# New state of the chunked RWKV scan: the old state's unit-matrix product on TensorE against a scaled copy on ScalarE and one fused VectorE instruction

## The chip, the cores and the metric

The kernel runs on one core of one Trainium2 chip. Its engines are TensorE (PE, matrix products; the loading of its stationary operand is listed apart as PEld), VectorE (DVE), ScalarE (ACT), GpSimd (POOL) and SyncE (SP, which here issues most DMAs). Each engine works through its own list of instructions in order, and engines wait for each other by semaphores. The metric is the device time of one execution in microseconds (us). The profile comes from one further execution, taken by the hardware profiler.

## What is computed

The program is a two-layer encoder over 1280 tokens (a prompt of 256 and a sample of 1024), 1024 channels, float32. Layer 0 mixes tokens by a bidirectional RWKV-7 recurrence, layer 1 by neighbourhood attention; each is followed by a squared-ReLU MLP. Only the recurrence matters here. For each head (64 channels) and each direction it is

```
def step(S, inp):
    r_t, w_t, k_t, v_t, a_t, b_t = inp
    sa = jnp.einsum('bhvk,bhk->bhv', S, a_t)
    S = S * w_t[:, :, None, :] + sa[..., None] * b_t[:, :, None, :] + v_t[..., None] * k_t[:, :, None, :]
    return S, jnp.einsum('bhvk,bhk->bhv', S, r_t)
```

The kernel does not go token by token. It takes chunks of 64 tokens: within a chunk, products of 64 x 64 matrices give the outputs and the new state S from the old one. If the inputs of a chunk are scaled by the running decay, the new state is D * (S + K'v + B'u), where D is the decay of the whole chunk (one number per key channel, thus one per partition), v are the values, u is the solution of a triangular system of the chunk, and K' and B' are the chunk's scaled keys.

## The kernel before

**Stages.** Layer 0's projections come first, then the preparation of scaled operands for the scan (written to DRAM as `ar_d` and `bk_d`), then the scan, then the MLP of layer 0, the attention and the MLP of layer 1. The scan's recurrence runs from about 738 us to 1378 us of the span.

**Jobs and units.** The scan has ten jobs (`jobs`). Jobs 0 and 1 hold the prompt (four head pairs of 4 chunks each), jobs 2 to 9 hold one head pair of the sample each (16 chunks). A head pair fills the 128 partitions: a helper `pair` (its matmul is line 976) issues each product twice, for partitions 0 to 63 and 64 to 127, on two quarters of the array. A float32 product stands as two records per half in the trace, so one `pair` is four MATMUL records.

**The planner's clock.** All work of the scan is entered by `at(t, f)` with a due time t in units; job j starts at 16 j, and a unit holds one chunk forward (d = 0) and one chunk backward (d = 1, 0.481 later). `scan_until` sorts all entries by due time and emits them under a manual schedule, so each of PE, DVE, ACT and POOL executes its instructions exactly in that order. The due time sets the order only; the clock on the chip is whatever the engines make of it.

**A step of the recurrence** is `scan_step`, in four parts at t - 0.68, t, t + 0.33 and t + 0.66. They work in a PSUM tile `wu` per direction with three regions `w`, `us`, `sn`:

- `s0`: `w` = zk v.
- `s1`: `w` += ar S (the old state); ACT copies `w` to `up` (line 997); `yo` += zk v.
- `s2`: `yo` += ar S; `sn` = lt v (line 1006); `sn` += I S, the unit matrix `ident` times the old state (lines 1007 and 1008, in the trace `wu<-S,cst`); `us` = Q up; ACT copies `us` to `u` (line 1011).
- `s3`: `sn` += lt u; ACT writes the new state S = D * `sn` (line 1019, `dall` holds D); `yo` += zb u. Every fourth chunk of d = 1, DVE takes the output `yo` out (lines 1026 and 1028).

The next chunk's `s1`, 0.34 units after `s3`, is the first reader of the new state.

**What else runs in these units.** DVE masks the products of the coming chunks (`zk` line 928 and, after an ACT copy of the same PSUM tile at line 814, `zb` line 815) and normalises outputs (`scan_post`: sums, an inverse square root with two ACT steps at lines 1121 and 1122, lines 1053 to 1073 and 1109 to 1125), with three large tensor operations of it on POOL. Above all it inverts the triangular systems of the next job by 31 rank-one updates (`rank1`, lines 853 and 855: tmp = column * row, q += tmp). They are due from -16.24 of their own job, that is from -0.24 of the job that is scanned at the time, in batches every half unit, over about ten units. After them ACT transposes q (`qst`, line 868), SP stores it, loads it back in another layout (`qld`, lines 886 and 891) and goes on with the loads of `ar` (line 801) that stand behind in its queue.

Of the kernel before, what the change touches and what calls it, by code (L numbers as in the profile page):

```python
# [5 lines left out]
F32 = mybir.dt.float32  # L6
F32R = mybir.dt.float32r
AF = mybir.ActivationFunctionType
ALU = mybir.AluOpType
# [4 lines left out]
P = 128  # L14
# [4 lines left out]
L = 64  # L19
# [29 lines left out]
class Trunk:  # L49
# [722 lines left out]
    def at(self, t, f, level=3):  # L772
        self.todo.append((t, len(self.todo), f, level))
# [196 lines left out]
    def half(self, e):  # L970
        return slice(64 * e, 64 * e + 64)
# [6 lines left out]
    def scan_step(self, at, t, J, st, d, cc, m, ch, new, end, i, last):  # L978
        nc = self.nc
        g, c = cc // 4, cc % 4  # L980
        R = {}
        w, us, sn = (lambda s=s: self.pbank[d][:, s] for s in (slice(0, L), slice(L, 2 * L), slice(2 * L, 3 * L)))
        yb = lambda: self.ybank[i // 4 % 2]
        yo = lambda: yb()[:, int(g > 1), c, :]
        half = self.half

        def s0():
            zk, vt = J["zk"][d, g], J["vt"]
            self.pair(lambda e, z: (w()[z], zk[z, c, 0:64], vt[z, 0, cc, :]))

        def s1():
            ar, zk, vt = J["ar"][d, g], J["zk"][d, g], J["vt"]
            S = R["S"] = None if new else st["S"]
            if S is not None:
                self.pair(lambda e, z: (w()[z], ar[z, c, 0:64], S[z]), start=False, free=True)
            up = R["up"] = self.sp.tile([P, L], F32, name="up", tag="up", bufs=4)
            nc.scalar.copy(up, w())
            self.pair(lambda e, z: (yo()[half(1 - e)], zk[z, c, 64:128], vt[z, 0, cc, :]), start=d == 0 and i % 4 == 0, free=True)

        def s2():  # L1000
            Q, up, S, ar, vt = J["Q"], R["up"], R["S"], J["ar"][d, g], J["vt"]
            if S is not None:
                self.pair(lambda e, z: (yo()[half(1 - e)], ar[z, c, 64:128], S[z]), start=False, free=True)
            if not end:
                lt = J["lt"][d, g]
                self.pair(lambda e, z: (sn()[z], lt[z, c, 1, :], vt[z, 0, cc, :]), start=False, free=True)
                if S is not None:
                    self.pair(lambda e, z: (sn()[z], self.ident[z, z], S[z]), start=False, free=True)
            self.pair(lambda e, z: (us()[z], Q[z, cc, d, :], up[z]), start=last, free=True)
            u = R["u"] = self.sp.tile([P, L], F32, name="u", tag="u", bufs=4)  # L1010
            nc.scalar.copy(u, us())

        def s3():
            u, zb, y = R["u"], J["zb"][d, g], J["y"]
            if not end:
                lt = J["lt"][d, g]
                self.pair(lambda e, z: (sn()[z], lt[z, c, 0, :], u[z]), start=False, free=True)
                S2 = self.sp.tile([P, L], F32, name="S", tag="S", bufs=5)
                nc.scalar.activation(S2, sn(), AF.Copy, scale=self.dall[:, m, d, ch:ch + 1])
                st["S"] = S2  # L1020
            self.pair(lambda e, z: (yo()[half(1 - e)], zb[z, c, 64:128], u[z]), start=False, free=True)
            if d == 1 and i % 4 == 3:
                lo = min(g, 3 - g)
                y = y.rearrange("p (x c) v -> p x c v", c=4)[:, lo:4 - lo:3 - 2 * lo]
                if i < 8:
                    nc.vector.tensor_copy(y, yb())
                else:
                    nc.vector.tensor_tensor(out=y, in0=yb(), in1=y, op=ALU.add)
        at(t - 0.68, s0)
        at(t, s1)  # L1030
        at(t + 0.33, s2)
        at(t + 0.66, s3)

    def scan_post(self, at, J, grp, last):
# [865 lines left out]
```

## Time and profile before

| | |
|---|---|
| median of 3 runs | 4070.0 us (4069.32 to 4076.52) |
| the profiled execution | 4072.58 us, its span 4070.8 us |
| mean granted TensorE clock over the span | 0.965 |
| the scan's recurrence, 738 to 1378 us | 640 us |

The profile lists busy time by engine, groups of equal instructions by line with their mean duration, what each engine waited for, and single instructions in order of time. "Busy" of PE is the union of modelled spans that overlap, so the distance from one matmul's start to the next says more about its price than its duration. All products of `pair` share line 976; they are told apart by their tiles (`wu<-S,cst` is out `wu`, moving operand S, stationary operand from the constants).

### The profile page before, as it was taken

The page shows a single profiled execution, that of the slowest core. Times are in us where ns is not written, and L with a number is a line of the kernel's source. Part 1 is how long each engine was busy: PE and PEld are TensorE (multiplying, and loading weights), DVE is VectorE, ACT ScalarE, POOL GpSimd, SP SyncE. Part 2 cuts the span into 40 slices and gives each one's busy share as a digit, 9 for nine tenths or more (in the row PEclk, how much of TensorE's full clock was granted, in tenths as well). Part 3 has the DMA queues.
Part 4 walks back from the last instruction along what each step waited for, and adds up shares of the span by engine and source line. Part 5 has one row for each costly group of instructions (what it writes and reads, how often), then busy time and mean ns, then how long its engine had stood idle before and what let it go on. Part 6 is the DMA issues. An engine that isn't in the chain of part 4 may idle for free.

```text
span 4070.8 us, 91014 instructions
## 1 busy us (share of the span) xinstructions
PE 3830.8 (94%) x36820; PEld 3236.5 (80%) x36820; DVE 2236.7 (55%) x4581; ACT 1582.2 (39%) x3868; POOL 1337.9 (33%) x1252
## 2 busy tenths in 40 slices
PE   8988988788888899999999999999989999999999
PEld 5765578688888788888888879887778888888888
DVE  5777742465665447555555562355554755555555
ACT  6776642455555531111111133456663211111111
POOL 4445542022221434222222241344442422222222
PEclk9987889899999999999999999999999999999999
DMA  4226564666664431111111115345464111111101
GB/s 142 71 101 213 195 213 128 161 160 161 154 166 117 138 109 37 42 37 37 42 37 37 42 51 165 115 106 113 94 171 157 42 37 37 42 37 37 42 32 63
DMA packets 450885, 394.89 MB, mean 97 GB/s; under 512 B 267456, under 2 KB 352832, under 8 KB 450464
## 3 DMA queue, kind: packets, MB, share of 16 engines
q1 hardware_dynamic: 416048, 327.72, 28.5%
q10 hardware_dynamic: 34416, 61.35, 4.2%
q8 instruction: 289, 4.73, 0.5%
q14 instruction: 132, 1.08, 0.1%
HBM read 270.50 MB, written 124.44 MB: 97 GB/s over the span
## 4 chain that ended last, share of the span: by engine, by line
PE 79%; DVE 6%; ACT 5%; DMA 4%; issue 3%; POOL 2%; SPq 1%; ACTq 0%; DVEq 0%; POOLq 0%
PE ps L95 19%; PE ps L96 19%; PE ps L97 18%; PE wu L976 4%; PE vps L510 2%; PE vps L512 1%; PE vps L511 1%; PE op L1815 1%; PE aps L976 1%; PE kps L976 1%; PE pt L1758 1%; PE lps L976 1%; DVE q L855 1%; PE yo L976 1%; PE yps L976 1%
## 5 line engine op out<-in xcount | busy, mean ns | idle before, releaser
L1361 DVE TENSOR_TENSOR x<-ps,x 128x256 f32<-128x256 f32 x1488 | 814.4, 594 | 645.3 <-PE ps L97 645.0
L95 PE MATMUL ps<-ah,whi 128*128 128x512 f32 (+1 forms) x2304 | 842.6, 366 | 0.0
L96 PE MATMUL ps<-al,whi 128*128 128x512 f32 (+1 forms) x2304 | 825.9, 358 | 0.0
L97 PE MATMUL ps<-ah,wlo 128*128 128x512 f32 (+1 forms) x2304 | 823.2, 357 | 1.7 <-DVE wlo L90 1.4
L90 POOL TENSOR_TENSOR wlo<-raw,whi 128x1024 fp32r<-128x1024 f32 (+1 forms) x178 | 390.6, 2195 | 855.5 <-ACT whi L89 831.1
L95 PE MATMUL ps<-hh,whi 128*128 128x512 f32 (+1 forms) x1536 | 547.8, 357 | 9.4 <-DVE x L1361 9.4
L96 PE MATMUL ps<-hl,whi 128*128 128x512 f32 (+1 forms) x1536 | 546.7, 356 | 0.0
L97 PE MATMUL ps<-hh,wlo 128*128 128x512 f32 (+1 forms) x1536 | 545.9, 355 | 0.0
L95 PEld LDWEIGHTS ps<-ah,whi 128*128 128x128 f32 x2304 | 434.3, 189 | 72.6 <-issue 8.0
L97 PEld LDWEIGHTS ps<-ah,wlo 128*128 128x128 f32 x2304 | 433.4, 188 | 72.2 <-DVE wlo L90 1.9
L96 PEld LDWEIGHTS ps<-al,whi 128*128 128x128 f32 x2304 | 434.5, 189 | 62.9 <-issue 1.0
L89 ACT CAST whi<-raw 128x1024 fp32r<-128x1024 f32 (+1 forms) x206 | 200.5, 973 | 713.7 <-PE ps L96 630.1
L1340 POOL TENSOR_TENSOR rl<-rl 128x512 f32<-128x512 f32 (+1 forms) x192 | 174.2, 907 | 505.7 <-PE ps L97 462.3
L95 PEld LDWEIGHTS ps<-hh,whi 128*128 128x128 f32 x1536 | 291.5, 190 | 54.0 <-DVE x L1361 11.4
L97 PEld LDWEIGHTS ps<-hh,wlo 128*128 128x128 f32 x1536 | 291.7, 190 | 41.8
L96 PEld LDWEIGHTS ps<-hl,whi 128*128 128x128 f32 x1536 | 291.4, 190 | 40.6
L1339 ACT ACTIVATE rl<-ps 128x512 f32<-128x512 f32 (+1 forms) x192 | 100.8, 525 | 555.6 <-PE ps L97 555.6
L1342 ACT CAST hh<-rl 128x512 fp32r<-128x512 f32 (+1 forms) x192 | 105.6, 550 | 324.1 <-POOL rl L1340 324.1
L1343 DVE TENSOR_TENSOR hl<-rl,hh 128x512 fp32r<-128x512 f32 (+1 forms) x192 | 119.8, 624 | 143.6 <-ACT hh L1342 143.2
L1752 POOL TENSOR_TENSOR s<-s,mx 128x384 f32<-128x384 f32 (+1 forms) x150 | 109.9, 746 | 162.9 <-DVE mx L1751 114.7
L976 PE MATMUL aps<-ar,bb 64*64 64x128 f32 x1280 | 117.9, 290 | 24.2 <-DMA ar<-ar_d 17.6
L1057 POOL TENSOR_TENSOR y<-y,mu 128x512 f32<-128x512 f32 x18 | 19.3, 1075 | 368.1 <-DVE mu L1054 341.5
(302 smaller groups left out, 8288.5 us busy)
## 6 DMA issues: line engine op xcount, KB each, us to landing
raw<-in_w_down_dram SPq DMA_DIRECT2D x64, 512.0 KB
raw<-in_w_up_dram SPq DMA_DIRECT2D x64, 512.0 KB
ar<-ar_d SPq DMA_DIRECT2D x80, 256.0 KB
bk<-bk_d SPq DMA_DIRECT2D x80, 256.0 KB
ar_d<-ar ACTq DMA_DIRECT2D x32, 512.0 KB
bk_d<-bk ACTq DMA_DIRECT2D x32, 512.0 KB
bs<-tab SPq DMA_DIRECT2D x128, 96.0 KB
v_d<-vt ACTq DMA_DIRECT2D x80, 128.0 KB
```

The costliest lines, as they stand in the source:

```text
L89: nc.scalar.copy(hi[:, cs], raw)
L90: lo_eng.tensor_tensor(out=lo[:, cs], in0=raw, in1=hi[:, cs].bitcast(F32), op=ALU.subtract)
L95: mm(ps, sh, mh, start=first, stop=False)
L96: mm(ps, sh, ml, start=False, stop=False)
L97: mm(ps, sl, mh, start=False, stop=last)
L976: self.nc.tensor.matmul(out, w, x, start=start, stop=stop, skip_group_check=free)
L1339: nc.scalar.activation(r[:, :n], ps[:, :n], AF.Relu)
L1340: nc.gpsimd.tensor_tensor(out=r[:, :n], in0=r[:, :n], in1=r[:, :n], op=ALU.mult)
L1342: nc.scalar.copy(hh[:, :n], r[:, :n])
L1343: nc.vector.tensor_tensor(out=hl[:, :n], in0=r[:, :n], in1=hh[:, :n].bitcast(F32), op=ALU.subtract)
L1361: nc.vector.tensor_tensor(out=xv, in0=ps[:, :n], in1=xv, op=ALU.add)
L1752: nc.gpsimd.tensor_tensor(out=s[:, :nk], in0=s[:, :nk], in1=mx[:, 2:3].to_broadcast([P, nk]), op=ALU.mult)
```

## The change

The unit-matrix product leaves TensorE. In `s2` ScalarE multiplies the old state in SBUF by D into a new tile `sd` (three buffers, 128 x 64). In `s3` VectorE makes the new state: D times `sn`, plus `sd`, in one scalar_tensor_tensor instruction; where there is no old state (a first chunk), it is D times `sn` alone. ScalarE's instruction of line 1019 goes.

```
             if not end:
                 lt = J["lt"][d, g]
                 self.pair(lambda e, z: (sn()[z], lt[z, c, 1, :], vt[z, 0, cc, :]), start=False, free=True)
-                if S is not None:
-                    self.pair(lambda e, z: (sn()[z], self.ident[z, z], S[z]), start=False, free=True)
+            if S is not None and not end:
+                sd = R["sd"] = self.sp.tile([P, L], F32, name="sd", tag="sd", bufs=3)
+                nc.scalar.activation(sd, S, AF.Copy, scale=self.dall[:, m, d, ch:ch + 1])
             self.pair(lambda e, z: (us()[z], Q[z, cc, d, :], up[z]), start=last, free=True)
...
                 S2 = self.sp.tile([P, L], F32, name="S", tag="S", bufs=5)
-                nc.scalar.activation(S2, sn(), AF.Copy, scale=self.dall[:, m, d, ch:ch + 1])
+                if R["S"] is None:
+                    nc.vector.tensor_scalar(out=S2, in0=sn(), scalar1=self.dall[:, m, d, ch:ch + 1], scalar2=None, op0=ALU.mult)
+                else:
+                    nc.vector.scalar_tensor_tensor(out=S2, in0=sn(), scalar=self.dall[:, m, d, ch:ch + 1], in1=R["sd"], op0=ALU.mult, op1=ALU.add)
                 st["S"] = S2
```

Over the ten jobs this is 256 unit-matrix products (chunks with an old state and a successor), 256 new ScalarE instructions, and 288 new states that pass from ScalarE to VectorE (32 of them without an old state).

## Prediction

> **What bounds the kernel now.** I read the page's busy times first, then busy time by stretch for the scan, because only the scan is touched. Columns of the second fence: stretch, length, then busy time (and instructions) of PE, PEld, DVE, ACT, POOL, granted clock, DMA share, GB/s.
>
> ```profile
> span 4070.8 us, 91014 instructions
> ...
> PE 3830.8 (94%) x36820; PEld 3236.5 (80%) x36820; DVE 2236.7 (55%) x4581; ACT 1582.2 (39%) x3868; POOL 1337.9 (33%) x1252
> ```
>
> ```profile
> 738.00:1378.00 640.00, 561.27 (x18613) 521.99 (x18609) 365.37 (x914) 371.84 (x1387) 154.06 (x174) 0.97 0.60 148
> ```
>
> Over the scan PE seems to be the bound: 561 of 640 us, DVE only 365. But the rank-one updates fill ten of a job's sixteen units, so I cut the scan at their first and last instruction: nine stretches with them (742 to 776, 805 to 840 and so on to 1265 to 1301), eight without them between these, and the end. The two sum rows are of the nine and of the eight.
>
> ```profile
> 742.00:776.00 34.00, 31.17 (x1012) 29.54 (x1012) 25.66 (x71) 18.12 (x71) 0.00 (x0) 0.95 0.61 154
> ...
> 999.00:1038.00 39.00, 35.86 (x1176) 34.06 (x1178) 32.02 (x82) 20.65 (x80) 7.93 (x9) 0.94 0.58 143
> 1067.00:1104.00 37.00, 33.41 (x1165) 31.44 (x1163) 31.75 (x82) 20.55 (x80) 8.04 (x10) 1.00 0.61 157
> ...
> sum 329.00, PE 301.30 PEld 284.18 DVE 277.70 ACT 178.16 POOL 64.61; mean PE 33.48 PEld 31.58 DVE 30.86 ACT 19.80 POOL 7.18
> ```
>
> ```profile
> 1104.00:1133.00 29.00, 24.27 (x785) 22.45 (x779) 7.76 (x20) 17.68 (x62) 7.05 (x9) 0.94 0.69 159
> ...
> sum 230.00, PE 189.57 PEld 174.01 DVE 62.26 ACT 141.23 POOL 57.62; mean PE 23.70 PEld 21.75 DVE 7.78 ACT 17.65 POOL 7.20
> ```
>
> ```profile
> 1301.00:1378.00 77.00, 68.20 (x2395) 61.95 (x2392) 24.75 (x48) 49.55 (x190) 31.84 (x30) 1.00 0.39 116
> ```
>
> The reader is to see two regimes. With rank-one updates DVE is busy 278 of 329 us (84%), nearly as much as PE. Without them it is busy 62 of 230 (27%). Single instructions of one such stretch, of DVE, ACT, POOL and PE, show how near its limit DVE is (start, duration, and in brackets idle time before it and what ended it):
>
> ```profile
> 1008.36 1.10 POOL L1057 TENSOR_TENSOR y<-y,mu 128x512 f32<-128x512 f32 x1 [10.32 <-DVE mu L1054]
> 1008.59 1.10 DVE L855 TENSOR_TENSOR q<-q,tmp 128x207 f32<-128x207 f32 x1
> 1009.73 0.39 DVE L853 TENSOR_TENSOR tmp<-mt,q 128x220 f32<-128x220 f32 x1
> ...
> 1010.68 0.38 ACT L814 COPY zb<-aps 128x256 f32<-128x256 f32 x1
> ...
> 1012.21 0.42 DVE L815 TENSOR_TENSOR zb<-aps,cst 128x256 f32<-128x256 f32 x1
> 1012.54 0.41 DVE L853 TENSOR_TENSOR tmp<-mt,q 128x247 f32<-128x247 f32 x1
> ...
> 1016.70 0.21 ACT L1121 ACTIVATE rqt<-rqx 128x8 f32<-128x8 f32 x1 [1.49 <-DVE rqx L1109]
> ...
> 1020.71 0.28 PE L976 MATMUL kps<-ar,bk 64*64 64x128 f32 x2
> ...
> 1022.84 0.68 DVE L928 TENSOR_TENSOR zk<-kps,cst 128x512 f32<-128x512 f32 x1
> ...
> 1027.98 0.42 DVE L815 TENSOR_TENSOR zb<-aps,cst 128x256 f32<-128x256 f32 x1 [1.89 <-ACT zb L814]
> ```
>
> DVE starts `zb` at 1012.21, though ACT was done at 1011.06: 1.15 us late. It starts `zk` at 1022.84, though the product ended at 1020.99: 1.85 us late. ACT stands still 1.49 us for DVE's `rqx`. Only at 1027.98 does DVE wait again. So from some 1008 to 1027 DVE trails by 1.0 to 1.9 us, partly because an update that takes 0.39 takes 1.10 beside a POOL instruction (1008.59). Today this lag is harmless: `zk` and `zb` are needed units later.
>
> **The change, part by part.**
>
> ```profile
> 1042.03 0.28 PE L976 MATMUL wu<-v,lt 64*64 64x64 f32 x4
> 1042.14 0.28 PE L976 MATMUL wu<-S,cst 64*64 64x64 f32 x4
> 1042.26 0.28 PE L976 MATMUL wu<-up,qq 64*64 64x64 f32 x4
> ```
>
> *Unit-matrix product removed.* It holds PE from 1042.14 to 1042.26, 0.115 us; 256 of them are 29.4 us of PE's stream. That is the most the change can give by itself.
>
> *ScalarE.* The groups by line and the waits within the scan:
>
> ```profile
> L1019 ACT ACTIVATE S<-wu,dall 128x64 f32<-128x64 f32 x288 | 92.4, 321 | 41.8 <-PE wu L976 40.9
> ...
> L928 DVE TENSOR_TENSOR zk<-kps,cst 128x512 f32<-128x512 f32 x79 | 54.3, 687 | 51.5 <-PE kps L976 51.4
> ...
> L815 DVE TENSOR_TENSOR zb<-aps,cst 128x256 f32<-128x256 f32 x63 | 26.5, 421 | 84.6 <-ACT zb L814 84.6
> ...
> L1125 DVE SCALAR_TENSOR_TENSOR rqr<-rqt,rqr 128x8 f32<-128x8 f32 x19 | 3.2, 167 | 0.6
> ```
>
> ```profile
> ACT u L1011 <- PE wu L976: 112.2, 206, 2.6
> ```
>
> 288 instructions of 321 ns go and 256 come; the trace has none like them (SBUF source), so I take the same 0.32 us, from 0.21 (the small SBUF activation at 1016.70) to 0.38 (the copy at 1010.68). They stand ahead of the `u` copy, where ACT waits for PE in 206 of 320 chunks (ten jobs of 32), 0.54 us each on average: hidden, cost nothing. Without that cover it would be up to 0.3 us in the other third.
>
> *VectorE's new state.* Not in the trace. The two rows from PSUM give (687 - 421)/256 = 1.04 ns an element, thus an estimate of 0.22 us for 64; bounds are 0.17 (the 8-element instruction of line 1125) and 0.42 (line 815). A follower starts 0.09 us before such an instruction ends (1012.21 + 0.42 against 1012.54), so a place in the queue costs 0.08 to 0.33, and I take 0.18.
> The Trainium skill (Perfetto Trace Analysis, Optimizing Scalar/DVE Operations) puts the access overhead at about 125 ns for VectorE on PSUM against 51 for ScalarE, and a profiled latency at about twice the overhead. By it, as an estimate, 0.32 us would stand for the new state (250 ns plus 67), and 0.52 for line 815, where the trace has 0.42: the measurement decides, and that price would only move the latency by 0.1 us.
>
> *Order.* This decides. The new state is due at 0.66 and 1.141 of each unit, among rank-one batches, masks and normalisation, and behind it wait `ar` S of the next chunk and all of PE's later work. How late may it be?
>
> ```profile
> 1005.09 0.32 ACT L1019 ACTIVATE S<-wu,dall 128x64 f32<-128x64 f32 x1 [0.29 <-PE wu L976]
> ...
> 1005.81 0.22 PE L976 MATMUL wu<-S,ar 64*64 64x64 f32 x1
> ```
>
> It ends at 1005.41 and is used at 1005.81: 0.4 us. VectorE's is 0.1 shorter, the removed product took 0.115 of that time: still 0.4. A lag of 1.0 to 1.9 us, take 1.5, no longer fits. DVE's queue from 1.14 to 5.14 units of a job (masks, normalisation of the job before, eight batches) is full already and gets eight new states, 8 x 0.18 = 1.4. PE then trails its old time by 1.5 + 1.4 - 0.4 = 2.5 us. The later half unit batches are about PE's pace, so I let nothing be won or lost there. Bounds for a stretch: -2.0 (17 products of 0.115, everything hidden) and +4.1 (lag 1.9, 0.33 each, no more slack than 0.4).
>
> *Stretches without updates.* Twelve products, 1.4 us each, if PE sets the pace. It does not always (a DVE and an SP instruction, then two pieces of the chain that ended last):
>
> ```profile
> 1038.04 0.19 DVE L855 TENSOR_TENSOR q<-q,tmp 128x31 f32<-128x31 f32 x1
> ...
> 1041.12 0.32 SPq L870 DMA_DIRECT2D qd<-qt  x1
> ...
> 1052.45 4.75 DMA ar<-ar_d
> ...
> 1057.34 0.29 PE aps L976 x2
> ```
>
> From the last update SP needs until 1052.45 to get through the stores and reloads of q to the next `ar` load, and PE waits for its landing. A faster PE waits longer there. I take half, -0.7.
>
> *No DMA is added, removed or moved.* But the last update ends later where DVE is the bound, and this chain starts later with it; that is inside the 2.5.
>
> **Sum.** Eight full stretches, 8 x 2.5 = +20.0. Eight without, 8 x -0.7 = -5.6. The stretch at 742, with DVE busy 26 of 34 us and POOL idle: some 9 products, -1.0. The end from 1301, with DVE busy 25 of 77: 40 products of 0.115, -4.6. Together +8.8 us. The profiled execution's 4072.6 becomes 4081.4; it stands 2.6 us above the median of the runs, so against 4070.0 I expect **4079 us**, +0.2%. (A measurement of this kernel can tell about 0.2%, 8 us, from no change.)
>
> **Rivals.**
> 1. *VectorE keeps up and PE's saving arrives: faster.* For it: PE is busy 88% of the scan, and DVE's busy time in full stretches, 31 of 37 us, has room for 18 x 0.18 = 3.2. The point from which it decides: the new state no later than 0.4 us after its sum, thus the lag gone. Price: -29.4 if all comes, about -18 with half of the stretches without updates lost and some latency: 4041 to 4062, middle 4052. Against it: the lag is there in the trace.
> The Trainium skill (Perfetto Trace Analysis, Identifying the Most-Contended Engine) would relieve the engine of highest occupancy, for TensorE by LDWEIGHTS: 522 of 640 us here against DVE's 365, which speaks for this rival. Its next section (Optimization Strategy) allows for regimes in which that engine changes; the sum rows above bear this out, 284 against 278.
> 2. *It cancels:* the lag drains within a stretch (DVE's idle 1.89 us at 1027.98 is room for it), loss 1.0 instead of 2.5: 8 x 1.0 - 11.2 for the three other terms = -3, thus 4067; 4062 to 4078.
> 3. *Worse:* the waits come singly, DVE idles for each sum and then is late again, each full stretch +4.1 and nothing won between: 8 x 4.1 - 1.0 - 4.6 = +27, 4097; up to 4110.
> 4. *The change does not do what it says:* the order is written out, so the products vanish; a new wait of `wu`'s next writer for VectorE's read of the same tile would be rival 3.
>
> **Chances.** Forecast (4078 to 4092) 0.39, rival 1 0.25, rival 2 0.28, rivals 3 and 4 0.08. Faster by over 0.2% 0.25, within 0.28, slower 0.47. The range 4050 to 4097 leaves out the far half of rival 1 and the end of rival 3; the forecast's own range is 4078 to 4092.
>
> **What would show it.** In the new profile: 256 x 4 `wu<-S,cst` records gone; PE and its weight load waiting for DVE `S` in place of ACT `S`, 2 us and more in each full stretch; these stretches some 2 us longer, the others a little shorter, the end 4 to 5 us shorter; `zb` and `zk` lags near zero, since DVE may no longer trail. Wrong, if the waits for DVE `S` stay under 1 us a stretch (then rival 1 or 2), or if ACT's `u` copies come late behind the new scaled copies.

## The result, and the profile after

The changed kernel takes 4082.51 us (median of 9 runs, 4076.69 to 4088.65), the kernel before 4069.32 (9 runs, 4055.43 to 4076.52): a ratio of 1.0042 (95% interval 1.0030 to 1.0053). The change makes the kernel slower, by some 13 us. The profiled execution took 4086.37 us, 13.8 more than that of before.

The page of the changed kernel, its busy times first, as for the kernel before:

```profile
span 4084.2 us, 89250 instructions
...
PE 3809.8 (93%) x35796; PEld 3204.7 (78%) x35796; DVE 2299.2 (56%) x4869; ACT 1559.5 (38%) x3836; POOL 1332.8 (33%) x1252
```

The matmul records fall by 36820 - 35796 = 1024, which is 256 products of four: the unit-matrix products are gone, and PE is busy 21 us less. DVE has 288 instructions more and is busy 62.5 us more. Neither sum tells that the span grew by 13.4 us. For that the scan has to be cut where its regime changes. The next two fences are busy time by stretch, first of the changed kernel, then of the kernel before (columns as in the prediction: stretch, length, busy time of PE, PEld, DVE, ACT, POOL, granted clock, DMA share, GB/s). The cuts are now the exact first and last rank-one update of each job. The sum with the larger DVE time is of the eight full stretches (updates of jobs 2 to 9), the other of the eight stretches between them, and the last row is the end.

```profile
863.12:907.65 44.53, 37.88 (x1144) 34.76 (x1144) 36.61 (x102) 19.51 (x79) 8.08 (x10) 0.89 0.52 135
933.80:974.34 40.54, 33.84 (x1144) 30.25 (x1144) 35.99 (x102) 19.27 (x79) 7.39 (x9) 1.00 0.57 141
1000.48:1042.07 41.59, 34.90 (x1144) 31.63 (x1144) 35.98 (x102) 19.19 (x79) 7.43 (x10) 0.96 0.55 140
...
1276.21:1318.05 41.84, 35.34 (x1064) 32.74 (x1064) 34.35 (x97) 18.04 (x74) 7.38 (x9) 0.84 0.27 61
sum 334.35, PE 281.92 PEld 256.94 DVE 286.78 ACT 151.02 POOL 61.73; mean PE 35.24 PEld 32.12 DVE 35.85 ACT 18.88 POOL 7.72
...
sum 213.91, PE 165.67 PEld 146.64 DVE 75.16 ACT 132.17 POOL 56.22; mean PE 20.71 PEld 18.33 DVE 9.39 ACT 16.52 POOL 7.03
...
1318.05:1393.40 75.35, 65.27 (x2184) 59.36 (x2180) 32.19 (x88) 47.14 (x186) 31.64 (x30) 0.93 0.39 117
```

```profile
867.47:905.99 38.52, 35.76 (x1199) 33.80 (x1201) 32.38 (x84) 20.61 (x81) 7.94 (x9) 0.96 0.59 151
933.54:970.87 37.33, 33.90 (x1182) 31.88 (x1184) 32.47 (x84) 20.61 (x81) 7.94 (x9) 1.00 0.63 157
...
1264.92:1301.80 36.88, 33.32 (x1119) 31.84 (x1121) 31.51 (x79) 18.93 (x76) 8.24 (x10) 0.91 0.31 78
sum 304.03, PE 277.18 PEld 261.56 DVE 260.61 ACT 162.24 POOL 66.95; mean PE 34.65 PEld 32.69 DVE 32.58 ACT 20.28 POOL 8.37
...
sum 221.12, PE 183.11 PEld 167.81 DVE 53.85 ACT 139.26 POOL 55.28; mean PE 22.89 PEld 20.98 DVE 6.73 ACT 17.41 POOL 6.91
...
1301.80:1377.33 75.53, 67.07 (x2358) 60.96 (x2352) 23.98 (x46) 49.12 (x188) 31.84 (x30) 1.00 0.39 115
```

The full stretches grew from 304.0 to 334.4 us, +30.3, though PE has fewer instructions in each (in the second of them 1144 records against 1199). DVE is busy 286.8 of their 334.4 us. Of the 30.3 us, 26.2 are DVE's busy time (260.6 to 286.8) and 4.1 its idle time. The stretches without updates shrank by 7.2, the end by 0.2 and the stretch of job 0 (34.92 to 34.28) by 0.6. Together the scan is 22.3 us longer. The rest of this execution, whose code did not change, was 8.9 us shorter than in the profiled execution of before; so 13.4 is left of the span.

Who waits, within the scan of the changed kernel (engine, tile and line, what it waited for: us in total, times, longest):

```profile
ACT u L1012 <- PE wu L976: 93.8, 157, 1.7
...
PEld wu L976 <- DVE S L1023: 71.9, 95, 1.8
PE wu L976 <- DVE S L1023: 49.5, 77, 1.6
DVE zb L815 <- ACT zb L814: 40.4, 39, 1.9
...
ACT rqt L1125 <- DVE rqx L1113: 23.0, 19, 2.1
```

Before, PE and its weight load waited for the new state 3.3 and 8.2 us in the scan:

```profile
PEld wu L976 <- ACT S L1019: 8.2, 25, 2.0
...
PE wu L976 <- ACT S L1019: 3.3, 5, 1.9
```

Now it is 49.5 and 71.9. (The two overlap in time, so their sum is no loss of time.) In one full stretch, that at 1000, they are 5.6 and 7.8, about as much as in the whole scan before:

```profile
PEld wu L976 <- DVE S L1023: 7.8, 9, 1.8
PE wu L976 <- DVE S L1023: 5.6, 7, 1.6
```

All of PE's waits for line 1023 stand at the first reader of the new state (`wu<-S,ar`), none at the product that writes `wu` next. DVE in that stretch, one instruction after the other (start, duration):

```profile
1009.85 0.28 DVE L1023 SCALAR_TENSOR_TENSOR S<-wu,dall,sd 128x64 f32<-128x64 f32 x1
1010.05 1.23 DVE L853 TENSOR_TENSOR tmp<-mt,q 128x207 f32<-128x207 f32 x1
1011.32 0.38 DVE L855 TENSOR_TENSOR q<-q,tmp 128x207 f32<-128x207 f32 x1
...
1012.46 0.28 DVE L1023 SCALAR_TENSOR_TENSOR S<-wu,dall,sd 128x64 f32<-128x64 f32 x1
...
1020.67 1.15 DVE L855 TENSOR_TENSOR q<-q,tmp 128x255 f32<-128x255 f32 x1
1021.74 0.27 DVE L1023 SCALAR_TENSOR_TENSOR S<-wu,dall,sd 128x64 f32<-128x64 f32 x1
1021.93 0.67 DVE L1030 COPY y<-yo 128x512 f32<-128x512 f32 x1
1022.53 0.84 DVE L853 TENSOR_TENSOR tmp<-mt,q 128x256 f32<-128x256 f32 x1
1023.40 1.37 DVE L855 TENSOR_TENSOR q<-q,tmp 128x256 f32<-128x256 f32 x1
1024.69 0.41 DVE L815 TENSOR_TENSOR zb<-aps,cst 128x256 f32<-128x256 f32 x1
1025.03 0.27 DVE L1023 SCALAR_TENSOR_TENSOR S<-wu,dall,sd 128x64 f32<-128x64 f32 x1
```

No row here has an idle time in brackets: DVE does not wait in them. From the new state at 1021.74 to the next at 1025.03 are 3.3 us, with an output copy, the two instructions of an update and a mask between them; one of the two takes 1.37 us. A new state can't be made out of turn, so its reader on PE waits for what stands ahead of it: 1.59 us for the state of 1025.03, and for that of 1012.46

```profile
1012.79 0.27 PE L976 MATMUL wu<-S,ar 64*64 64x64 f32 x2 [1.14 <-DVE S L1023]
```

POOL at the same times:

```profile
1010.01 1.04 POOL L1061 TENSOR_TENSOR y<-y,mu 128x512 f32<-128x512 f32 x1 [9.49 <-DVE mu L1058]
...
1020.44 1.09 POOL L1086 TENSOR_TENSOR y<-y,rqr 128x512 f32<-128x512 f32 x1 [2.83 <-DVE rqr L1129]
1021.61 1.48 POOL L1091 TENSOR_TENSOR y<-y,lnx 128x256 f32<-128x256 f32 x2
1023.16 1.32 POOL L1094 TENSOR_TENSOR y<-y,vb 128x512 f32<-128x512 f32 x1
```

Each of the update instructions of 0.84 to 1.37 us lies beside one of these; that at 1011.32, with POOL idle, takes 0.38. The new state at 1021.74 lies wholly inside POOL's 1021.61 to 1023.09 and still takes its usual 0.27. The Trainium skill (SBUF — State Buffer, Who interferes with whom) says that a VectorE instruction with two SBUF inputs contends with a GpSimd instruction that reads SBUF, and that one with at most one such input does not, outside some faster modes: by that rule the new state itself (PSUM and `sd`) is not lengthened, only what stands ahead of it. The rows above agree.

Over all 140 new states of the full stretches I worked out from the trace's records how long after the last product of `sn` VectorE (before: ScalarE) began the new state: 0.14 us on average before, 0.79 after. The time from its end to the first product that reads it fell from 0.58 to 0.16, and 92 of 140 such products began within 0.12 us of it, where there had been 20. The reserve of 0.4 us in the prediction, taken from one row, is used up, and the lag is on the path.

### The profile page after: what moved, and what is told of

It is laid out like the page before. It is cut to its first block, busy times and chain, and to the rows that moved or that the text cites. A ratio compares the mean times of both kernels' runs of the same rounds, so it can differ in the third digit from the quotient of the medians.

```text
span 4084.2 us, 89250 instructions
## 1 busy us (share of the span) xinstructions
PE 3809.8 (93%) x35796; PEld 3204.7 (78%) x35796; DVE 2299.2 (56%) x4869; ACT 1559.5 (38%) x3836; POOL 1332.8 (33%) x1252
## 4 chain that ended last, share of the span: by engine, by line
PE 73%; DVE 8%; ACT 5%; DMA 5%; issue 5%; POOL 3%; SPq 1%; ACTq 0%; DVEq 0%; POOLq 0%
PE ps L95 19%; PE ps L96 18%; PE ps L97 18%; PE wu L976 2%; DVE tmp L853 1%; PE vps L510 1%; PE vps L511 1%; PE vps L512 1%; PE op L1819 1%; PE pt L1762 1%; DVE q L855 1%; DMA dd<-zb 1%; PE aps L976 1%; DMA mraw<-dd 1%; PE nst L1561 1%
## 5 line engine op out<-in xcount | busy, mean ns | idle before, releaser
L95 PEld LDWEIGHTS ps<-hh,whi 128*128 128x128 f32 x1536 | 291.0, 189 | 53.9 <-DVE x L1365 11.4
L853 DVE TENSOR_TENSOR tmp<-mt,q 128x31 f32<-128x31 f32 (+15 forms) x310 | 120.7, 389 | 42.6 <-issue 12.7
```

The source lines that it names most:

```text
L95: mm(ps, sh, mh, start=first, stop=False)
L853: nc.vector.tensor_tensor(out=tv, in0=mt[:, 0:jj, jj:jj + 1].to_broadcast([P, jj, w]), in1=q[:, jj:jj + 1, jj:].to_broadcast([P, jj, w]), ...
```

## The experiments

Three theories were put to the test. Theory 1, the queue: in the full stretches the new state stands behind VectorE's in-order work, lengthened beside GpSimd. Theory 2: ScalarE's scaled copies delay the `up` and `u` copies. Theory 3: the step itself became longer everywhere, by latency. The stretches named in the table are those of each run's own profiled execution; each ratio is against the kernel before on the same chip. Runs c and d have no updates by which to cut the scan.

| run | median us (before) | ratio, interval | full | without | end |
|---|---|---|---|---|---|
| before | | | 304.0 | 221.1 | 75.5 |
| the change | 4082.5 (4069.3) | 1.0042, 1.0030 to 1.0053 | 334.4 | 213.9 | 75.4 |
| a: product gone, S on ACT | 4056.9 (4067.8) | 0.9976, 0.9966 to 0.9986 | 296.8 | 219.2 | 72.6 |
| b: product kept, S on DVE | 4087.2 (4067.8) | 1.0049, 1.0035 to 1.0064 | 333.0 | 216.7 | 76.1 |
| c: before, no updates | 4054.7 (4067.8) | 0.9970, 0.9961 to 0.9979 | | | |
| d: the change, no updates | 4039.8 (4067.8) | 0.9929, 0.9914 to 0.9944 | | | |
| e: the change, no POOL steps | 4059.2 (4068.3) | 0.9973, 0.9958 to 0.9987 | 310.2 | 213.4 | 75.9 |
| f: before, no POOL steps | 4065.1 (4068.3) | 0.9989, 0.9978 to 0.9999 | 305.4 | 221.3 | 76.2 |
| g: by regime | 4060.6 (4068.3) | 0.9976, 0.9966 to 0.9986 | 309.5 | 213.3 | 74.8 |
| h: as i, job 8 later too | 4083.3 (4068.3) | 1.0035, 1.0023 to 1.0048 | 317.7 | 219.9 | 84.2 |
| i: the change, normalisation later | 4076.8 (4065.9) | 1.0031, 1.0020 to 1.0042 | 316.0 | 221.2 | 79.5 |
| k: before, normalisation later | 4081.6 (4065.9) | 1.0039, 1.0025 to 1.0053 | 311.9 | 231.5 | 80.2 |

**a and b take the change apart.** Run a leaves the product out and keeps the new state on ScalarE (the old state's own part is then missing from the sum):

```
                 self.pair(lambda e, z: (sn()[z], lt[z, c, 1, :], vt[z, 0, cc, :]), start=False, free=True)
-                if S is not None:
-                    self.pair(lambda e, z: (sn()[z], self.ident[z, z], S[z]), start=False, free=True)
```

> The kernel before without the unit-matrix product, the new state still on ScalarE. It leaves the old state's own part out of the new state. All theories grant 256 x 0.115 = 29 us of TensorE's stream; the question is how much of it is on the path. If TensorE sets the pace of the scan: 4040 to 4054 us, full stretches (with rank-one updates) 1.5 to 2 us shorter each, the end from 1301 some 4 us shorter. If the scan is paced by latencies from engine to engine: within 8 us of 4069, and the end not shorter.

Run b keeps the product and moves only the new state; there is no scaled copy:

```
-                nc.scalar.activation(S2, sn(), AF.Copy, scale=self.dall[:, m, d, ch:ch + 1])
+                nc.vector.tensor_scalar(out=S2, in0=sn(), scalar1=self.dall[:, m, d, ch:ch + 1], scalar2=None, op0=ALU.mult)
```

> The kernel before with one edit: the new state is made by VectorE (decay times sum), the product stays on TensorE, no scaled copy on ScalarE. Theory 1 (VectorE's queue is full of rank-one updates and the new state waits behind them): full stretches 3 to 5 us longer each, 4095 to 4110 us. Theory 2 (the scaled copies on ScalarE, ahead of the u copies, are what costs): no loss, 4062 to 4072. Theory 3 (a new state from VectorE is later everywhere, by its own latency): stretches without updates and the end grow as well, in proportion to their chunks.

Run a gained 10.9 us of medians, between its two expectations, so it does not tell whether TensorE or the latencies from engine to engine set the pace of the scan. Run b lost 19.3: its full stretches grew by 3.6 us each, as expected by theory 1, but the time stayed below the 4095 to 4110 expected, in part because the stretches without updates shrank by 4.4 in sum. The full stretches of a and of b, busy time by stretch, their sums:

```profile
sum 296.75, PE 268.04 PEld 250.69 DVE 259.84 ACT 161.11 POOL 66.27; mean PE 33.51 PEld 31.34 DVE 32.48 ACT 20.14 POOL 8.28
```

```profile
sum 332.97, PE 288.05 PEld 264.38 DVE 285.88 ACT 127.05 POOL 60.58; mean PE 36.01 PEld 33.05 DVE 35.73 ACT 15.88 POOL 7.57
```

With the product kept and ScalarE relieved of 35 us (162.2 to 127.1), b's full stretches are as long as those of the change (333.0 against 334.4). Theory 2 falls as the cause of the loss: b has no scaled copies at all and loses as much. That the full stretches of b and of the change are equal, though only the change is rid of the product, can mean that the product is worth nothing where VectorE sets the pace, or that the scaled copies cost about what it saves; no run has the copies alone. The move to VectorE carries the whole loss, and the product, by itself, was worth 7 us in the full stretches of the kernel before and 11 in all, of the 29.4 us that it took of PE's stream.

**c and d take VectorE's load away.** Both leave out the rank-one updates (the triangular systems stay without their inverse), c in the kernel before, d in the changed one:

```
-                tmp = self.er.tile([P, 256], F32, name="tmp", tag="tmp", bufs=2)
...
-                nc.vector.tensor_tensor(out=q[:, 0:jj, jj:], in0=q[:, 0:jj, jj:], in1=tv, op=ALU.add)
```

> The kernel before without the rank-one updates on VectorE (the triangular inverses stay unit matrices); the base for the next run. VectorE is then busy about a quarter of the scan. No theory needs a number here; by the idle time of the stretches I expect 3980 to 4060 us.

> The changed kernel without the rank-one updates. Compared with the run before it (the old kernel without them). Theory 1: the loss is gone, 8 to 25 us faster than that run. Theory 2 (ScalarE's scaled copies): still 8 us and more slower. Theory 3 (latency of the new state on VectorE): within 8 us or slower.

Without the updates the change is a gain: 4039.8 against 4054.7, 15 us; the two intervals (0.9914 to 0.9944, 0.9961 to 0.9979) don't touch. In the scan of d, PE's wait for the new state is what was left of it with VectorE nearly free:

```profile
PE wu L971 <- DVE S L1018: 11.4, 32, 0.6
```

0.6 us is the longest, against 1.6, and 11.4 the sum, against 49.5. Theory 3 falls with this: where no updates stand in the way the new step is the shorter one. What d does not tell is whether the number of the updates or their lengthening beside GpSimd makes the queue.

**e and f take GpSimd away.** The five GpSimd steps of the normalisation (ahead of the prediction I had counted three) are left out in all jobs but the last (those outputs stay without their normalisation), e in the changed kernel, f in the kernel before:

```
-                at(t0 + dt, f)
+                if last or f not in (p2, p3b, p4, p4b, p5):
+                    at(t0 + dt, f)
```

> The changed kernel without the normalisation's five GpSimd steps in all jobs but the last (outputs stay unnormalised). Rank-one updates then no longer stretch from 0.4 to 1.1 us beside GpSimd, about 3 us of VectorE's time in each full stretch. Theory 1: full stretches some 2 to 3 us shorter than in the changed kernel, 16 to 24 us in all, 4058 to 4068. If lag behind GpSimd is not what the new states wait for: within 8 us of 4082.

> The kernel before without the same five GpSimd steps. Theory 1: VectorE's lag is covered here, so full stretches shorten by 1 us or less each, 4061 to 4070. If the changed kernel gains no more from this than the kernel before does, the share of GpSimd in the loss is nothing.

The full stretches of e, then of f:

```profile
sum 310.22, PE 277.50 PEld 252.57 DVE 259.33 ACT 150.95 POOL 4.20; mean PE 34.69 PEld 31.57 DVE 32.42 ACT 18.87 POOL 0.53
```

```profile
sum 305.37, PE 275.21 PEld 260.04 DVE 235.63 ACT 163.16 POOL 4.20; mean PE 34.40 PEld 32.51 DVE 29.45 ACT 20.40 POOL 0.53
```

DVE's busy time falls by 27.5 us with the change (286.8 to 259.3) and by 25 without it (260.6 to 235.6). The same relief is worth 24 us of full stretches in the changed kernel and nothing in the one before (its full stretches were 1.3 us longer), where VectorE's lag had no follower. With GpSimd's steps gone the change is 5.9 us ahead by medians, though the intervals of e and f overlap. So most of the loss needs both, the updates and the work on GpSimd. With GpSimd's steps both the lengthening of the updates and VectorE's own waits for GpSimd's tiles go. No run parts the two, but the traces do: inside the full stretches no idle time of VectorE of 0.15 us or more is ended by GpSimd, with the change or in e, while the instructions of the updates take 193.7 us in sum with the change (the longest 1.37) and 167.5 in e (the longest 0.43). So of the two it is the lengthening. In e the new states still begin 0.61 us after their last product on average, where the change has 0.79, and the stretches lose only 5 us over f: the time lost does not follow the mean lag.

**h, i and k move GpSimd's work instead of dropping it.** In h the second half of each job's normalisation is due six units later, out of the updates, in all jobs but the last:

```
-            t0 = (12.5, 17.496)[half]
+            t0 = (12.5, 17.496 if last else 23.496)[half]
```

> The changed kernel, with one edit: the second half of each job's output normalisation (all but the last job's) is due six units later, so it leaves units 1 to 5 of the next job, where VectorE also has the larger rank-one updates, for units 7 to 11. Theory (new states wait behind bursts in VectorE's queue): VectorE's work is the same, but the burst is flatter, full stretches 1 to 2.5 us shorter than in the changed kernel, 4062 to 4075. If only VectorE's total work counts: within 4 us of the changed kernel's 4082.

It took 4083.3 us, no better than the change, as its second expectation had it. But its full stretches were shorter (317.7 us), and the end was 84.2: job 8's late normalisation now fell into the last job. So h decided nothing, and i is h with job 8 at its old due times; k is the same move in the kernel before.

```
-            t0 = (12.5, 17.496)[half]
+            t0 = (12.5, 23.496 if grp is not self.jobs[-2] and not last else 17.496)[half]
```

> As the last kernel with the later normalisation, but job 8 keeps its old due times, so the last job isn't held up (there the end grew by 9 us). If the bursts beside the rank-one updates are what the new states wait for: full stretches as short as in that run (318 us in sum against 334 of the changed kernel), the end back at 75 us, 4070 to 4076. If the time only moves: 4080 to 4084 again.

> The kernel before with the same later due times of the normalisation. Its new states are on ScalarE, so nothing waits for VectorE's queue in full stretches: within 5 us of 4069. If it gains as much as the changed kernel does, the later due times help by another way than the new states' wait.

The full stretches of i, then of k:

```profile
sum 315.99, PE 271.82 PEld 249.35 DVE 263.49 ACT 144.90 POOL 25.64; mean PE 33.98 PEld 31.17 DVE 32.94 ACT 18.11 POOL 3.21
```

```profile
sum 311.86, PE 271.99 PEld 254.94 DVE 238.57 ACT 156.03 POOL 25.79; mean PE 34.00 PEld 31.87 DVE 29.82 ACT 19.50 POOL 3.22
```

The move alone cost the kernel before 15.8 us (4081.6 against 4065.9), where I had expected next to nothing: in its profiled execution 10 us more in the stretches without updates, 8 more in the full ones and 5 in the end. Why it costs so much was not followed up. What the pair does show is the same as e and f: with GpSimd's work mostly out of the updates (POOL busy 26 us there instead of 62), the change loses 4 us in the full stretches instead of 30, and by medians is 4.9 us ahead, again with overlapping intervals. As a cure the move is worth nothing: i has the short full stretches that were expected of it, but its end came back only to 79.5, not to 75, and its time, 4076.8, is just above the 4070 to 4076 expected.

**g uses each form where it pays.** Units 0 to 9 of jobs 1 to 8, where the updates stand, keep the old step; units 10 to 15, the first job and the last take the new one (as an edit of the kernel before; the scaled copy and the new state follow `dve` too):

```
+        dve = i >= 10 or J["j"] in (0, 9)
...
-                if S is not None:
+                if S is not None and not dve:
                     self.pair(lambda e, z: (sn()[z], self.ident[z, z], S[z]), start=False, free=True)
```

> The changed step only where VectorE has no rank-one updates beside it (units 10 to 15 of jobs 1 to 8, and jobs 0 and 9); elsewhere the step of before. If the loss comes from the full stretches alone, they return to 304 us in sum (before) and the stretches without updates keep their gain of some 7 us: 4058 to 4066 against 4069. If the gain of the stretches without updates only exists because longer full stretches let the stores and loads between them get done, it goes: 4066 to 4073.

It took 4060.6 us against 4068.3 of the kernel before, 0.9976 (0.9966 to 0.9986), faster than both kernels. Its sums, full stretches and those without updates:

```profile
sum 309.52, PE 280.26 PEld 263.61 DVE 260.80 ACT 162.10 POOL 66.76; mean PE 35.03 PEld 32.95 DVE 32.60 ACT 20.26 POOL 8.34
...
sum 213.32, PE 171.73 PEld 154.44 DVE 70.55 ACT 133.05 POOL 55.45; mean PE 21.47 PEld 19.31 DVE 8.82 ACT 16.63 POOL 6.93
```

The stretches without updates keep the whole gain of the change (-7.8 us), and the full ones lose 5.5 us instead of 30. Their new states are all on ScalarE, as before; why they did not come back to 304 us, as expected, is open.

## Why the prediction was right, and where its sizes were off

The predicted time was 4079 us, the measured one 4082.5. The direction, the mechanism (a new state that waits in VectorE's queue) and the place (the full stretches) were those of the forecast. That the total came so near is in part luck; the sum met it only in part by its own terms:

| term | predicted | profiled executions |
|---|---|---|
| eight full stretches | 8 x 2.5 = +20.0 | +30.3 (8 x 3.8) |
| eight without updates | -5.6 | -7.2 |
| stretch at job 0 | -1.0 | -0.6 |
| end | -4.6 | -0.2 |
| scan together | +8.8 | +22.3 |
| outside the scan | 0 | -8.9 |

The scan came out 13.5 us worse than the sum. In the profiled executions the unchanged rest hides two thirds of that, which no term foresaw: over the kernels of the table whose scan can be cut, the rest takes from 3420 to 3435 us, and the kernel before happens to have the longest. The medians differ by 13.2 us.

- **Bound by stretch, not by engine.** Right, though in the prediction's own sums the weight load still stood ahead of DVE in the full stretches (284 to 278 us); only with the change does DVE lead there (287 to 257). Over the scan DVE is busy 424 of 663 us, and still it sets the pace of half of it:

```profile
731.00:1394.00 663.00, 545.54 (x17607) 492.25 (x17602) 423.93 (x1203) 349.50 (x1355) 149.59 (x174) 0.95 0.58 143
```

- **Unit-matrix product.** At most 29.4 us; 10.9 came (run a); the whole change brought 15 where VectorE was free (d against c).
- **ScalarE's scaled copies cost nothing.** Supported, but not to the microsecond. Their duration was 0.35 us instead of the 0.32 taken, and ACT's waits for PE ahead of `u` are still there, 93.8 us in 157 chunks (112.2 in 206 before), so there is cover. By the trace's records the `u` copies of the full stretches begin 0.19 us after their last product on average, 0.16 in b, which has no scaled copies, and 0.15 before; so they do not come late behind the copies by more than some 0.03 us. From b to the change, which drops the product and adds the copies, the loss over before falls from 19.3 to 13.2 us; a, which drops the product alone, gains 10.9. The difference of 5 us is about what these medians leave open.
- **VectorE's instruction.** I took 0.22 us for its duration and 0.18 for its place in the queue. All instructions of the two lines (count, then shortest, median and longest in ns):

```profile
L1009 ACT ACTIVATE sd<-S,dall x256: 331/351/403, 740.6 to 1391.1; 128x64 f32<-128x64 f32 x128
...
L1023 DVE SCALAR_TENSOR_TENSOR S<-wu,dall,sd x256: 269/283/286, 742.3 to 1392.1; 128x64 f32<-128x64 f32 x128
```

  It is 0.283 us, and its follower starts 0.19 to 0.20 after it (1009.85 to 1010.05, 1021.74 to 1021.93). The estimate by the Trainium skill (Perfetto Trace Analysis, Optimizing Scalar/DVE Operations), 0.32, was nearer to the duration than mine from the row; the price in the queue, which counts where DVE is the bound, was right, but by luck: 0.22 less the 0.09 of overlap would have been 0.13, and I gave no reason for 0.18.
- **Order.** Right in kind and mis-sized: this is the term that failed, 2.5 us a stretch against 3.8. I charged eight of a stretch's eighteen states (fourteen in the first) to DVE's queue and let PE run on after them at no loss. The runs show all of them charged: DVE's busy time grew by 26 us in these stretches (260.6 to 286.8), about what 140 new states of 0.19 make, 27 us, thus 3.3 a stretch, and its idle time by 0.5 a stretch. I read the idle time so that each late state also makes PE late with what DVE needs next: inside the full stretches DVE's longer idle times that PE ended are 15.6 us in sum, 9.6 before. That is not tested by a run. In e and f the same states cost 24 us of DVE and only 5 of time: the busy time counts where DVE has no room left. The upper bound of +4.1 held the mean but not the stretches at 863 and 1276, which grew by 6.0 and 5.0 us; they show granted clocks of 0.89 and 0.84, those of before 0.96 and 0.91.
- **Stretches without updates.** -0.9 each against -0.7. Part of it is not the product: a, without the product, gained 1.9 us there, and b, with the product and the state on VectorE, 4.4. With ACT relieved these stretches get shorter too, which the prediction had not considered.
- **End.** -0.2 against -4.6. Run a gained 2.9 here, b lost 0.5, and g, with the new step in the whole last job, gained 0.8: the product was worth less than its stream, and the state on VectorE gave most of that back. The change's own end had a granted clock of 0.93, all of a, b and before 1.00, so part of the miss may be that.
- **What would show it.** The waits of PE for DVE's `S` were predicted at 2 us and more a stretch; it was 5.6 in the one shown. DVE's lag for `zb` was to go to near zero. It did not throughout: ScalarE's copy in the changed kernel

```profile
1023.04 0.38 ACT L814 COPY zb<-aps 128x256 f32<-128x256 f32 x1
```

  ended at 1023.42 and `zb` began at 1024.69, still 1.27 us late. DVE does trail, only PE now trails with it.

**The rivals.** That VectorE keeps up was decided by the point named, the lag: without the updates (d) the gain of 15 us came, close to the 18 of that rival's middle. That it cancels is what e and f show with GpSimd out of the way, +5 in the full stretches and -8 in the others. The worse case, +4.1 in each full stretch, was nearer to the truth there than the forecast's 2.5, but the stretches between did win. The new wait that rival 4 names, of `wu`'s next writer for VectorE, did not come: PE waits for the new state only where it reads it.

## What to carry to other kernels

Before an operation on the serial path moves to an engine that is idle on average, look at that engine in the stretches where its other work is dense, and at what stands directly ahead of the new place in its order: a lag that costs nothing while the queue holds only work needed later becomes the price of every step. Where the regimes differ, use each form in its own regime: here the change as a whole cost 0.42%, and the same change kept out of the updates gained 0.24%. An engine's lengthened instructions (here from 0.4 to as much as 1.4 us beside GpSimd) may be left out of account only as long as nothing on the path stands behind them.

## What the runs showed of the hardware that I had not expected

- The scaled copy from SBUF on ScalarE took 0.355 us on average, while the same copy out of PSUM had taken 0.321 in the kernel before.
- The granted clock was lower with the change in six of the eight full stretches: 0.89 in the stretch at 863 and 0.84 in the last one, 0.96 and 0.91 before. It is not a rule of this case (the longer stretch at 933, 40.54 against 37.33 us, had 1.00 in both). The clock by itself does not make the loss: over the eight stretches it is 0.93 on average with the change and 0.97 before, but 0.95 both in b, whose stretches are as long as with the change, and in e, whose stretches are 23 us shorter than b's.
- The execution outside the scan differed by 8.9 us between two profiled executions with the same code there, as much as the whole sum of the prediction. So the total of one execution can't decide a change of this size. Stretches of one regime say more, though each kernel's were seen in one execution only.
